# RWKV layer: r read from PSUM by its users, and the first half's preparation issued per head pair beside the r projection

## The chip, the cores and the metric

The kernel runs on one core of a Trainium2 chip. The metric is the device time of one execution in microseconds (us). A core has five engines that run their own queues in order and wait for each other by semaphores: TensorE (PE, with its weight loads PEld), VectorE (DVE), ScalarE (ACT), GpSimd (POOL) and SyncE (SP), which issues the loads.

## The reference, cut to what matters

The program is a chain of two blocks on 512 tokens of width 1024: an RWKV-7 time mix, an MLP, an attention layer, a second MLP, and then a block with a gated delta rule, latent attention and experts. Only the RWKV time mix is touched by the change. It has 16 heads of 64.

```
r, k, v = xr @ wr, xk @ wk, xv @ wv
decay = exp(-exp(w_log));  a = sigmoid(...)
kk = k * k_k, normalised per head
k  = k * (1 + (a - 1) * k_a)
for t:  S = S diag(decay_t) + (S (-kk_t)) (kk_t a_t)^T + v_t k_t^T;   y_t = S r_t
bonus = sum over a head of (r * k * r_k)
```

The recurrence is computed in eight chunks of 64 tokens. Within a chunk a triangular matrix of key products per head is inverted, so that the chunk's steps become matrix products.

## The kernel before, in words

Everything is feature-major: a tile of 128 partitions by 512 tokens holds two heads, a head pair p of 0 to 7. A projection goes through `dense_fm`, which for each p loads 128 columns of the weight, splits them into a high part on ScalarE (L181) and a low part on VectorE (L183), and issues 24 matmuls (L244 to L246) into one PSUM bank. The bank is handed to a function `use`.

For the r projection `use_r` keeps one pair back and calls `make_r` (L656 and on) on the pair before. `make_r` copies r from PSUM to SBUF on ScalarE (L659), makes the decay factors W and 1/W with two exponentials (L664, L666), and then the operands of the pair. On VectorE: kkn (L671, which reads the spread norm from PSUM), kp (L677), the bonus product of r (L679), and for each half of the sequence (four chunks) the two parts of `ar` (L689 from kkn, L690 from r). On GpSimd: kka (L673) and the two parts of `bk` (L691, L692). `sum_bonus` (L652) multiplies the bonus product on TensorE.

After the projection the weights' pool is closed, a pool `rwb` opens in its room, and `prepare(0)` runs over the eight pairs of the first half (chunks 0 to 3). For each pair: two modulation steps (`self.spare(2)`, a load of 512 KB from SP and matmuls L342, transposes L345 on VectorE); eight score matmuls (L729) into two PSUM banks; masks that write the scores into the matrix tile `GB` (L738, VectorE) and into the operands (L749 on VectorE, or L751 on ScalarE and L752 on GpSimd); a scaled copy of `bk` (L761 on ScalarE or L756 on GpSimd), its transposes (L765) and a copy out of PSUM (L767). Then the matrices are transposed in 32x32 blocks (L777), and the diagonal blocks of all 16 heads are inverted in 62 small steps (L783, L785), on VectorE in the first half and on GpSimd in the second. After that come transposes back (L793, L796) and block products on TensorE (L801, L808). `prepare(1)` does the same for chunks 4 to 7. Its pairs and inverse are traced behind everything else (`self.behind(100000)`) and write their matrix with L741 on ScalarE and L742 and L743 on GpSimd. The chunk loop (L902 to L939) follows; chunk 4 needs the second half's blocks.

PSUM has eight banks: five of tag "b", two of tag "f", one of tag "m" (modulation). In this layer `self.ps()` gives a "b" bank; under `behind` it gives an "f" bank. SBUF tiles of 128x512 come from one pool of 59 slots. A scheduler fixes each engine's order when the program is built: it issues what is ready by its own estimate of time, the earlier traced first.

Of the kernel before, what the change touches and what calls it, by code (L numbers as in the profile page):

```python
# [122 lines left out]
class K:  # L123
# [392 lines left out]
    def rwkv(self, x_dram, G, sh, gt, xT):  # L516
        nc, tc, A = self.nc, self.tc, self.A
        C0 = float(_np.exp(-0.5))
        self.open_weights(1024)
        rstd = self.rstd_fm(xT)  # L520
        hT, xx = [], []
        for k in range(KT):
            t = self.s()
# [113 lines left out]
        AR = [[None, None] for _ in range(8)]  # L637
# [17 lines left out]

        def make_r(p, pt):  # L656
            rB = spr(p)
            r = self.s()
            nc.scalar.activation(r, pt, AF.Copy)  # L659
            cum, aa = CA[p]  # L660
            CA[p] = None
            W = self.wp.tile([128, 8, 65], F32, name=self.nm("W"), tag="w65")
            nc.gpsimd.memset(W[:, :, 0:1], 1.0)
            nc.scalar.activation(W[:, :, 1:65], cum.rearrange("p (c t) -> p c t", t=64), AF.Exp, scale=-C0)  # L664
            Wi = self.s()
            nc.scalar.activation(Wi, cum, AF.Exp, scale=C0)  # L666
# [12 lines left out]
            nc.vector.scalar_tensor_tensor(prod, r, self.col("rw_rk", p), kp, op0=OP.mult, op1=OP.mult)  # L679
            prods.append((p, prod))  # L680
            if p:
                sum_bonus(*prods.pop(0))
            v3 = lambda x, hf: x[:, hf * 256:hf * 256 + 256].rearrange("p (c t) -> p c t", t=64)
            for hf in range(2):
                ar, bk = self.s(), self.s()
                AR[p][hf], BK[p][hf] = ar, bk
                a4, b4 = (z.rearrange("p (c t) -> p c t", t=128) for z in (ar, bk))
                cs = slice(hf * 4, hf * 4 + 4)
                nc.vector.scalar_tensor_tensor(a4[:, :, 0:64], v3(kkn, hf), -1.0, W[:, cs, 0:64], op0=OP.mult, op1=OP.mult)  # L689
                nc.vector.tensor_tensor(a4[:, :, 64:128], v3(r, hf), W[:, cs, 1:65], op=OP.mult)  # L690
                nc.gpsimd.tensor_tensor(b4[:, :, 0:64], v3(kka, hf), v3(Wi, hf), op=OP.mult)  # L691
                nc.gpsimd.tensor_tensor(b4[:, :, 64:128], v3(kp, hf), v3(Wi, hf), op=OP.mult)  # L692

        self.dense_fm(A["rw_wr"], xr, 0, D, use_r)
# [6 lines left out]
        gm = self.cst("gmask")  # L701
        idn = self.cst("ident")
        Y = [[None, None] for tt in range(4)]
        with tc.tile_pool(name="rwb", bufs=2, side="right", reuse_waits="tile") as bp:
            def new_sv(c):
# [4 lines left out]
                    out.append(t)  # L710
                return out

            X, BKt, GB = [None, None], [None, None], [None, None]

            def prepare(hf):
                eng = nc.gpsimd if hf else nc.vector
                GBh = bp.tile([128, 32, 128], F32, name=self.nm("GB"), tag="gb")
                Xh = [None] * 16
                Bh = [None] * 8
                for p in range(8):  # L720
                    g = p // 4
                    ar, bk = AR[p][hf], BK[p][hf]
                    self.spare(0 if hf else 2)
                    pts = [self.ps(), self.ps()]
                    for ci in range(4):
                        cs = slice(ci * 128, ci * 128 + 128)
                        for hd in range(2):
                            q = slice(hd * 64, hd * 64 + 64)
                            nc.tensor.matmul(pts[hd][:, cs], bk[q, cs], ar[q, cs], start=(ci == 0), stop=(ci == 3),  # L729
                                             skip_group_check=True)  # L730
                    xo = self.s()
                    nc.scalar.activation(xo[0:64], ar[64:128], AF.Copy)
                    for hd in range(2):
                        u0 = ((2 * p + hd) % 8) * 4
                        v = pts[hd].rearrange("p (c t) -> p c t", t=128)
                        o = GBh[g * 64:g * 64 + 64, u0:u0 + 4, :]
                        if hf == 0:
                            nc.vector.tensor_tensor(o, v[0:64], gm[0:64].unsqueeze(1).to_broadcast([64, 4, 128]), op=OP.mult)  # L738
                        else:

                            nc.scalar.activation(o, v[0:64], AF.Copy)  # L741
                            nc.gpsimd.memset(o[32:64, :, 0:32], 0.0)  # L742
                            nc.gpsimd.tensor_tensor(o[:, :, 64:128], o[:, :, 64:128],  # L743
                                                    gm[g * 64:g * 64 + 64, 64:128].unsqueeze(1).to_broadcast([64, 4, 64]), op=OP.mult)
                        dst = ar if hd == 0 else xo
                        d3 = dst[64:128].rearrange("p (c t) -> p c t", t=128)
                        mk = gm[64:128].unsqueeze(1).to_broadcast([64, 4, 128])
                        if hf == 0 and hd == 0:
                            nc.vector.tensor_tensor(d3, v[64:128], mk, op=OP.mult)  # L749
                        else:  # L750
                            nc.scalar.activation(d3, v[64:128], AF.Copy)  # L751
                            nc.gpsimd.tensor_tensor(d3, d3, mk, op=OP.mult)  # L752
                    Xh[2 * p], Xh[2 * p + 1] = ar, xo
                    dg = self.s()
                    if hf == 0 and p % 2:
                        nc.gpsimd.tensor_tensor(dg.rearrange("p (c t) -> p c t", t=128), bk.rearrange("p (c t) -> p c t", t=128),  # L756
                                                WCp[:, p, hf * 4:hf * 4 + 4].unsqueeze(2).to_broadcast([128, 4, 128]), op=OP.mult)
                    else:
                        for ci in range(4):
                            cs = slice(ci * 128, ci * 128 + 128)  # L760
                            nc.scalar.activation(dg[:, cs], bk[:, cs], AF.Copy, scale=WCp[:, p, hf * 4 + ci:hf * 4 + ci + 1])  # L761
                    pt = self.ps()
                    for ci in range(4):
                        cs = slice(ci * 128, ci * 128 + 128)
                        nc.tensor.transpose(pt[:, cs], dg[:, cs], idn)  # L765
                    Bh[p] = self.s()
                    nc.scalar.activation(Bh[p], pt, AF.Copy)  # L767

                P = bp.tile([128, 32, 32], F32, name=self.nm("P"), tag="p4", bufs=2)
# [25 lines left out]
                for ub in range(0, 32, 16):  # L797
# [15 lines left out]
                X[hf], BKt[hf], GB[hf] = Xh, Bh, GBh  # L813

            def finish(tt, g):

# [57 lines left out]
            step = lambda n, m: [next(z, None) for z in [gt8] * n + [bn8] * m]  # L874
            pr1 = prepare(1)
            with self.behind(100000, slots=False):
                next(pr1)
            SV = [new_sv(0), new_sv(1)]
            for g in range(2):
# [65 lines left out]
                        step(GA_[c], GB_[c])  # L945
            step(8, 8)
            del sv, us, z, zy


        self.need(1)  # L950
# [1463 lines left out]
```

## Time and profile before

| | |
|---|---|
| median of 3 runs | 3014.67 us (3011.07 to 3020.56) |
| the profiled execution's own time | 3021.37 us |
| its span in the profile | 3019.6 us |
| TensorE busy | 2778.8 us, 92% |
| VectorE / ScalarE / GpSimd busy | 1627.1 / 1051.5 / 732.4 us |
| mean granted TensorE clock | 0.952 |

Times in the rows are microseconds from the start of the span; the mean of one instruction in a group is in nanoseconds. "Idle before" is the time in which an engine had nothing running just ahead of the instructions of a group, with what ended it. PEclk is the granted clock of TensorE as a share of full speed. Matmuls are pipelined, so their busy times overlap.

### The profile page before, as it was taken

How to read it: one execution, taken by the hardware profiler on the slowest of the kernel's cores; microseconds unless marked ns; L12 is line 12 of the kernel's file. 1: busy time of each engine (PE TensorE's matmuls, PEld its weight loads, DVE VectorE, ACT ScalarE, POOL GpSimd, SP SyncE). 2: the span in 40 equal slices, each digit the busy share in tenths (PEclk: the TensorE clock that was granted, in tenths of full speed). 3: DMA queues.
4: the chain of work that ended last, by engine and by line, in shares of the span. 5: the costliest groups of instructions: out<-in, count | busy, mean ns of one | idle time of the engine just before them, and what ended most of it. 6: DMA issues, size and time to landing. Idle time of an engine off the chain costs nothing.

```text
span 3019.6 us, 38042 instructions
## 1 busy us (share of the span) xinstructions
PE 2778.8 (92%) x15046; PEld 1975.0 (65%) x15046; DVE 1627.1 (54%) x2449; ACT 1051.5 (35%) x1711; POOL 732.4 (24%) x563
## 2 busy tenths in 40 slices
PE   5998888999999999999999998898799997999997
PEld 1665466788877777788886776666677884444433
DVE  4568855456673447566536779638765542112112
ACT  2454533422234457432223452253335322110001
POOL 2446453211111034121113453134242121000000
PEclk8997777999999999999999999999999998999999
DMA  6322514256573321455532324142253359899998
GB/s 206 118 70 83 159 56 163 89 167 189 185 240 98 96 70 45 136 176 179 176 98 65 105 70 119 54 133 66 64 178 92 101 189 356 340 386 409 409 409 307
DMA packets 361011, 502.05 MB, mean 166 GB/s; under 512 B 24769, under 2 KB 236993, under 8 KB 360833
## 3 DMA queue, kind: packets, MB, share of 16 engines
q1 hardware_dynamic: 349600, 479.01, 46.9%
q10 hardware_dynamic: 11232, 20.62, 1.9%
q8 instruction: 118, 1.93, 0.3%
q14 instruction: 61, 0.49, 0.1%
HBM read 471.26 MB, written 26.21 MB: 165 GB/s over the span
## 4 chain that ended last, share of the span: by engine, by line
PE 68%; DVE 19%; DMA 5%; ACT 3%; issue 3%; POOL 2%; SPq 0%; ACTq 0%; DVEq 0%; POOLq 0%
PE psb L244 10%; PE psb L246 10%; PE psb L245 10%; PE psb L2114 5%; PE psb L1303 4%; PE psb L2142 4%; PE psf L1303 2%; DMA rg<-in_w_up_dram 2%; DMA rg<-in_w_gate_dram 1%; PE psb L1204 1%; PE psm L342 1%; DVE s L1465 1%; DVE tm L1380 1%; DVE R L1389 1%; DVE tm L1387 1%
## 5 line engine op out<-in xcount | busy, mean ns | idle before, releaser
L244 PE MATMUL psb<-s,wh 128*128 128x512 f32 x1384 | 543.6, 393 | 2.7 <-DVE s L968 1.9
L245 PE MATMUL psb<-s,wl 128*128 128x512 f32 x1384 | 541.6, 391 | 2.4 <-DVE wl L183 2.3
L246 PE MATMUL psb<-s,wh 128*128 128x512 f32 (+1 forms) x1320 | 514.8, 390 | 1.3 <-POOL s L481 0.6
L181 ACT ACTIVATE wh<-wr 128x1024 fp32r<-128x1024 f32 (+1 forms) x221 | 288.1, 1305 | 397.7 <-PE psb L246 263.9
L183 DVE TENSOR_TENSOR wl<-wr,wh 128x1024 fp32r<-128x1024 f32 (+1 forms) x145 | 257.2, 1775 | 262.9 <-ACT wh L181 259.5
L244 PEld LDWEIGHTS psb<-s,wh 128*128 128x128 f32 x1384 | 260.0, 188 | 70.9 <-issue 9.8
L245 PEld LDWEIGHTS psb<-s,wl 128*128 128x128 f32 x1384 | 259.9, 188 | 59.6 <-DVE wl L183 3.1
L246 PEld LDWEIGHTS psb<-s,wh 128*128 128x128 f32 (+1 forms) x1320 | 247.4, 188 | 58.0 <-issue 2.9
L183 POOL TENSOR_TENSOR wl<-wr,wh 128x1024 fp32r<-128x1024 f32 (+1 forms) x76 | 186.7, 2460 | 395.7 <-ACT wh L181 376.2
L2114 PE MATMUL psb<-rg,s 128*64 128x512 f32 x1024 | 242.9, 597 | 5.1 <-DMA rg<-in_w_up_dram 3.8
L1303 PE MATMUL psf<-f,wh 128*128 128x512 f32 (+1 forms) x688 | 232.0, 411 | 10.7 <-ACT wh L181 10.7
L999 POOL TENSOR_TENSOR s<-s 128x512 f32<-128x512 f32 x64 | 101.1, 1580 | 515.9 <-ACT s L997 436.6
L2114 PEld LDWEIGHTS psb<-rg,s 128*64 128x64 f32 x1024 | 83.0, 136 | 142.2 <-issue 120.7
L1303 PEld LDWEIGHTS psf<-f,wh 128*128 128x128 f32 (+1 forms) x688 | 133.2, 195 | 42.7 <-ACT wh L181 11.5
L1303 PE MATMUL psf<-f,wl 128*128 128x512 f32 (+1 forms) x344 | 143.1, 416 | 16.5 <-POOL wl L183 16.4
L2142 PE MATMUL psb<-rg,s 128*64 128x512 f32 (+1 forms) x544 | 129.6, 620 | 0.1
L378 DVE SCALAR_TENSOR_TENSOR mt<-mr,crep,mt 128x512 f32<-128x512 f32 x168 | 126.5, 753 | 3.6
L201 ACT ACTIVATE s<-s 128x512 fp32r<-128x512 f32 x112 | 69.7, 625 | 138.0 <-POOL s L999 73.2
L1006 DVE SCALAR_TENSOR_TENSOR s<-psb,aff,s 128x512 f32<-128x512 f32 x64 | 45.9, 751 | 129.7 <-PE psb L246 129.7
L1303 PE MATMUL psb<-f,wh 128*128 128x512 f32 (+1 forms) x336 | 106.4, 396 | 7.8 <-DVE f L479 5.9
L997 ACT ACTIVATE s<-psb 128x512 f32<-128x512 f32 x64 | 37.6, 588 | 164.0 <-PE psb L246 164.0
L2142 PEld LDWEIGHTS psb<-rg,s 128*64 128x64 f32 x544 | 46.1, 147 | 74.2 <-issue 68.8
(569 smaller groups left out, 4968.4 us busy)
## 6 DMA issues: line engine op xcount, KB each, us to landing
rg<-in_w_gate_dram SPq DMA_DIRECT2D x64, 1024.0 KB
rg<-in_w_up_dram SPq DMA_DIRECT2D x64, 1024.0 KB
rg<-in_w_down_dram SPq DMA_DIRECT2D x64, 1024.0 KB
mr<-in_mod_w_dram SPq DMA_DIRECT2D x96, 512.0 KB
wr<-in_mlp_down_dram SPq DMA_DIRECT2D x32, 1024.0 KB
wr<-in_mlp_up_dram SPq DMA_DIRECT2D x31, 1024.0 KB
wr<-in_w_in_dram SPq DMA_DIRECT2D x54, 512.0 KB
mr<-in_w_mod_dram SPq DMA_DIRECT2D x40, 512.0 KB
```

The costliest lines, as they stand in the source:

```text
L181: nc.scalar.activation(hi, raw, AF.Copy)
L183: (lo_eng or self.lo_eng or nc.vector).tensor_tensor(lo, raw, hi.bitcast(F32), op=OP.subtract)
L201: nc.scalar.activation(hi, src, AF.Copy)
L244: nc.tensor.matmul(pt[:mw], hi[k][:, j:j + mw], a, start=(k == 0), stop=False)
L245: nc.tensor.matmul(pt[:mw], lo[k][:, j:j + mw], a, start=False, stop=False)
L246: nc.tensor.matmul(pt[:mw], hi[k][:, j:j + mw], b, start=False, stop=(k == nk - 1))
L378: nc.vector.scalar_tensor_tensor(acc[:, hb], raw[:, d], c, acc[:, hb], op0=OP.mult, op1=OP.add)
L999: nc.gpsimd.tensor_tensor(sq, r, r, op=OP.mult)
L1006: nc.vector.scalar_tensor_tensor(xT[m], pt, gt[:, m:m + 1], xT[m], op0=OP.mult, op1=OP.add)
L1303: nc.tensor.matmul(pt[:rows, :cols], x, y, start=(k == 0 and q == 0), stop=(k == nk - 1 and q == 2))
L2114: nc.tensor.matmul(B[n][q], XE[hp][k0 // 2][:, o:o + 64], w[e][:, k, n * 512:n * 512 + 512], start=(k0 + k == 0), stop=(k0 + k == 7), skip ...
L2142: last = nc.tensor.matmul(pt[q, :n], HT[(k + i) // 4][:, o:o + 64], w[e][i], start=(k + i == 0), stop=(k + i == 7), skip_group_check=True)
```

## The change

Three things change in the RWKV layer, and two numbers elsewhere. `make_r` no longer copies r; L679 and the two L690 read the PSUM bank. The loop over pairs in `prepare` becomes a generator `pairs(hf, pool)`; the first half's generator is advanced by one pair after each `make_r` from the second on, so that six of its eight pairs are traced inside the r projection, and the last two behind it. Its score matmuls take "f" banks. The first half's matrix `GB` lies in a pool of its own, opened ahead of the weights' pool; `rwb` keeps one such buffer instead of two. The copy of the bonus comes after the eighth pair. The number of slots goes from 59 to 58, and the scratch for DMA descriptors from its default to 1 KB per partition.

```diff
     def rwkv(self, x_dram, G, sh, gt, xT):
+        gbm = tc.tile_pool(name="gb0", bufs=1, side="right", reuse_waits="tile")
+        gb0 = gbm.__enter__()
         self.open_weights(1024)
...
             if p:
                 make_r(*held.pop(0))
+            if p > 1:
+                prep[0].send(None)
...
             rB = spr(p)
-            r = self.s()
-            nc.scalar.activation(r, pt, AF.Copy)
...
-            nc.vector.scalar_tensor_tensor(prod, r, self.col("rw_rk", p), kp, op0=OP.mult, op1=OP.mult)
+            nc.vector.scalar_tensor_tensor(prod, pt, self.col("rw_rk", p), kp, op0=OP.mult, op1=OP.mult)
...
-                nc.vector.tensor_tensor(a4[:, :, 64:128], v3(r, hf), W[:, cs, 1:65], op=OP.mult)
+                nc.vector.tensor_tensor(a4[:, :, 64:128], v3(pt, hf), W[:, cs, 1:65], op=OP.mult)
...
+        def pairs(hf, pool):
+            GBh = GB[hf] = pool.tile([128, 32, 128], F32, name=self.nm("GB"), tag="gb", bufs=1)
...
+                self.spare(0 if hf else 2)
+                pts = [self.bank("f"), self.bank("f")]
...
+                Bh[p] = self.s()
+                nc.scalar.activation(Bh[p], pt, AF.Copy)
+                yield
+
+        prep = [pairs(0, gb0)]
         self.dense_fm(A["rw_wr"], xr, 0, D, use_r)
         make_r(*held.pop(0))
+        prep[0].send(None)
         sum_bonus(*prods.pop(0))
+        self.run(prep[0])
         nc.scalar.activation(bonus, pbon[:, 0:64].rearrange("p (c h) -> p c h", h=16), AF.Copy)
         self.close_weights()
...
             with self.behind(100000, slots=False):
+                self.run(pairs(1, bp))
                 next(pr1)
...
-            self.begin(st, 59)
+            self.begin(st, 58)
...
-    nc = _bacc.Bacc("TRN2", target_bir_lowering=False, num_devices=1)
+    nc = _bacc.Bacc("TRN2", target_bir_lowering=False, num_devices=1, dynamic_dma_scratch_size=1024)
```

What stands between these lines in `pairs` is the loop body of `prepare`, moved word for word.

## Rows read from the trace of the kernel before

**Rows 1.** The page: busy time of the engines, share of the span and instructions (first line), and the DMA queues that carry data with packets, megabytes and share of 16 engines.

```profile
PE 2778.8 (92%) x15046; PEld 1975.0 (65%) x15046; DVE 1627.1 (54%) x2449; ACT 1051.5 (35%) x1711; POOL 732.4 (24%) x563
...
q1 hardware_dynamic: 349600, 479.01, 46.9%
q10 hardware_dynamic: 11232, 20.62, 1.9%
```

**Rows 2.** Busy time by stretch: from to, length, busy us and instructions of PE, PEld, DVE, ACT, POOL, granted clock, DMA share, GB/s. The first stretch is the r projection's, the second the first half's preparation up to its inverse.

```profile
203.40:265.80 62.40, 53.05 (x249) 42.38 (x247) 59.37 (x73) 22.57 (x37) 47.18 (x52) 0.87 0.11 32
265.80:304.75 38.95, 32.78 (x211) 18.13 (x210) 27.09 (x38) 22.19 (x47) 19.77 (x20) 0.77 0.50 174
```

**Rows 3.** VectorE's groups by form from 203.4 to 304.75 us: line, operation, output and inputs, shapes, count, busy us, mean ns of one, idle before.

```profile
L690 DVE TENSOR_TENSOR s<-s,W 128x256 f32<-128x256 f32 x16 | 13.0, 813 | 0.0
L679 DVE SCALAR_TENSOR_TENSOR s<-s,P,s 128x512 f32<-128x512 f32 x8 | 11.1, 1388 | 0.4
L738 DVE TENSOR_TENSOR GB<-psb,C 64x512 f32<-64x512 f32 x16 | 10.8, 682 | 11.3 <-PE psb L729 11.1
...
L671 DVE SCALAR_TENSOR_TENSOR s<-s,P,psb 128x512 f32<-128x512 f32 x8 | 5.9, 743 | 0.4 <-PE psb L303 0.3
L749 DVE TENSOR_TENSOR s<-psb,C 64x512 f32<-64x512 f32 x8 | 5.6, 695 | 0.2
```

**Rows 4.** VectorE in order of time from the matrix transposes on: start, duration, instruction, count.

```profile
300.68 3.96 DVE L777 STREAM_TRANSPOSE P<-GB 32x1024 f32<-32x1024 f32 x2
304.75 0.20 DVE L783 TENSOR_TENSOR tm<-P,R 128x31 f32<-128x31 f32 x1
...
347.96 4.05 DVE L793 STREAM_TRANSPOSE TT<-R 32x1024 f32<-32x1024 f32 x2
...
368.26 3.86 DVE L777 STREAM_TRANSPOSE P<-GB 32x1024 f32<-32x1024 f32 x2 [3.02 <-PE psb L801]
```

**Rows 5.** GpSimd in order of time: the first and the last mask of the second half's pairs, and the first and the last step of the second half's inverse.

```profile
306.69 0.20 POOL L742 MEMSET GB<- 32x128 f32 x1 [2.56 <-ACT GB L741]
...
366.05 1.26 POOL L752 TENSOR_TENSOR s<-s,C 64x512 f32<-64x512 f32 x1
...
378.07 0.68 POOL L783 TENSOR_TENSOR tm<-P,R 128x31 f32<-128x31 f32 x1 [4.58 <-DVE P L777]
...
419.48 0.25 POOL L785 TENSOR_TENSOR R<-R,tm 128x31 f32<-128x31 f32 x1
```

**Rows 6.** The chain of work that ended last, in order of time: the last products of chunk 3 and the first of chunk 4.

```profile
415.18 1.09 PE psb L934 x16
...
437.54 0.84 PE psb L902 x12
```

**Rows 7.** Busy time by stretch, columns as in rows 2: dense stages behind the RWKV layer, and the end with the experts.

```profile
500.00:1000.00 500.00, 485.43 (x2160) 380.90 (x2161) 291.53 (x327) 168.57 (x195) 83.99 (x53) 0.99 0.52 166
...
2400.00:3019.00 619.00, 566.08 (x2597) 287.20 (x2595) 141.37 (x222) 98.53 (x153) 33.25 (x27) 0.96 0.89 345
```

**Rows 8.** VectorE in order of time in the r stage: two instructions of the same form.

```profile
219.00 0.41 DVE L690 TENSOR_TENSOR s<-s,W 128x256 f32<-128x256 f32 x1
...
224.16 0.94 DVE L690 TENSOR_TENSOR s<-s,W 128x256 f32<-128x256 f32 x1
```

**Rows 9.** GpSimd in order of time around these two.

```profile
217.56 0.91 POOL L692 TENSOR_TENSOR s<-s,s 128x256 f32<-128x256 f32 x1
219.48 0.12 POOL L663 MEMSET W<- 128x8 f32 x1 [1.01 <-DVE s L690]
...
223.92 0.91 POOL L691 TENSOR_TENSOR s<-s,s 128x256 f32<-128x256 f32 x1
```

**Rows 10.** VectorE's groups by form over the whole span: an instruction of another layer with a 128x256 input in PSUM.

```profile
L1180 DVE CUSTOM_DVE_ANT_0 s<-psb,mask 128x256 f32<-128x256 f32 x16 | 6.7, 417 | 10.5 <-PE psb L1175 10.5
```

**Rows 11.** TensorE in order of time: the first and the last matmul of one tile of a projection (of k; r's have the same form), the last of the third r tile, the first scores of the second half, a pair's bonus sums, and a modulation group, transposes and scores of one pair of the first half.

```profile
138.39 0.50 PE L244 MATMUL psb<-s,wh 128*128 128x512 f32 x1
...
143.78 0.40 PE L246 MATMUL psb<-s,wh 128*128 128x512 f32 x1
...
206.44 0.40 PE L246 MATMUL psb<-xl,wh 128*128 128x512 f32 x1
...
210.42 0.71 PE L729 MATMUL psf<-s,s 64*128 64x128 f32 x6
...
223.89 0.95 PE L652 MATMUL psb<-C,s 128*128 128x2 f32 x8
...
279.10 1.06 PE L342 MATMUL psm<-mr,crep 128*32 128x512 f32 x8
280.10 0.66 PE L765 MATMUL psb<-C,s 128*128 128x128 f32 x4
280.68 1.16 PE L729 MATMUL psb<-s,s 64*128 64x128 f32 x16
```

**Rows 12.** Waits of SyncE's queue from 150 to 440 us: line, what it waited for, total us, times, longest. L328 loads the modulation weights, L179 the projection weights.

```profile
SPq L328 <- PE psm L342: 101.1, 19, 48.9
SPq L179 <- DVE wl L183: 56.9, 9, 11.8
```

**Rows 13.** Waits from 203 to 270 us: ScalarE.

```profile
ACT W L664 <- DVE s L690: 30.4, 6, 6.1
```

**Rows 14.** ScalarE in order of time: the first copies of the second half's scores into its matrix.

```profile
266.45 1.05 ACT L741 ACTIVATE GB<-psf 64x512 f32<-64x512 f32 x2
```

More of the change, by code (lines that the diff above doesn't have):

```diff
@@ L689, in make_r @@
                 nc.vector.scalar_tensor_tensor(a4[:, :, 0:64], v3(kkn, hf), -1.0, W[:, cs, 0:64], op0=OP.mult, op1=OP.mult)
-                nc.vector.tensor_tensor(a4[:, :, 64:128], v3(r, hf), W[:, cs, 1:65], op=OP.mult)
+                nc.vector.tensor_tensor(a4[:, :, 64:128], v3(pt, hf), W[:, cs, 1:65], op=OP.mult)
                 nc.gpsimd.tensor_tensor(b4[:, :, 0:64], v3(kka, hf), v3(Wi, hf), op=OP.mult)
                 nc.gpsimd.tensor_tensor(b4[:, :, 64:128], v3(kp, hf), v3(Wi, hf), op=OP.mult)
+        gm = self.cst("gmask")
@@ new lines, in rwkv @@
+        idn = self.cst("ident")
+        X, BKt, GB = [None, None], [None, None], [None, None]
+        def pairs(hf, pool):
+            GBh = GB[hf] = pool.tile([128, 32, 128], F32, name=self.nm("GB"), tag="gb", bufs=1)
+            Xh = X[hf] = [None] * 16
+            Bh = BKt[hf] = [None] * 8
+            for p in range(8):
+                g = p // 4
+                ar, bk = AR[p][hf], BK[p][hf]
+                self.spare(0 if hf else 2)
+                pts = [self.bank("f"), self.bank("f")]
+                for ci in range(4):
+                    cs = slice(ci * 128, ci * 128 + 128)
+                    for hd in range(2):
+                        q = slice(hd * 64, hd * 64 + 64)
+                        nc.tensor.matmul(pts[hd][:, cs], bk[q, cs], ar[q, cs], start=(ci == 0), stop=(ci == 3),
+                                         skip_group_check=True)
+                xo = self.s()
+                nc.scalar.activation(xo[0:64], ar[64:128], AF.Copy)
+                for hd in range(2):
+                    u0 = ((2 * p + hd) % 8) * 4
+                    v = pts[hd].rearrange("p (c t) -> p c t", t=128)
+                    o = GBh[g * 64:g * 64 + 64, u0:u0 + 4, :]
+                    if hf == 0:
+                        nc.vector.tensor_tensor(o, v[0:64], gm[0:64].unsqueeze(1).to_broadcast([64, 4, 128]), op=OP.mult)
+                    else:
+                        nc.scalar.activation(o, v[0:64], AF.Copy)
+                        nc.gpsimd.memset(o[32:64, :, 0:32], 0.0)
+                        nc.gpsimd.tensor_tensor(o[:, :, 64:128], o[:, :, 64:128],
+                                                gm[g * 64:g * 64 + 64, 64:128].unsqueeze(1).to_broadcast([64, 4, 64]), op=OP.mult)
+                    dst = ar if hd == 0 else xo
+                    d3 = dst[64:128].rearrange("p (c t) -> p c t", t=128)
+                    mk = gm[64:128].unsqueeze(1).to_broadcast([64, 4, 128])
+                    if hf == 0 and hd == 0:
+                        nc.vector.tensor_tensor(d3, v[64:128], mk, op=OP.mult)
+                    else:
+                        nc.scalar.activation(d3, v[64:128], AF.Copy)
+                        nc.gpsimd.tensor_tensor(d3, d3, mk, op=OP.mult)
+                Xh[2 * p], Xh[2 * p + 1] = ar, xo
+                dg = self.s()
+                if hf == 0 and p % 2:
+                    nc.gpsimd.tensor_tensor(dg.rearrange("p (c t) -> p c t", t=128), bk.rearrange("p (c t) -> p c t", t=128),
+                                            WCp[:, p, hf * 4:hf * 4 + 4].unsqueeze(2).to_broadcast([128, 4, 128]), op=OP.mult)
+                else:
+                    for ci in range(4):
+                        cs = slice(ci * 128, ci * 128 + 128)
+                        nc.scalar.activation(dg[:, cs], bk[:, cs], AF.Copy, scale=WCp[:, p, hf * 4 + ci:hf * 4 + ci + 1])
+                pt = self.ps()
+                for ci in range(4):
+                    cs = slice(ci * 128, ci * 128 + 128)
+                    nc.tensor.transpose(pt[:, cs], dg[:, cs], idn)
+                Bh[p] = self.s()
+                nc.scalar.activation(Bh[p], pt, AF.Copy)
+                yield
@@ L694, in rwkv @@
+        prep = [pairs(0, gb0)]
         self.dense_fm(A["rw_wr"], xr, 0, D, use_r)
         make_r(*held.pop(0))
+        prep[0].send(None)
         sum_bonus(*prods.pop(0))
+        self.run(prep[0])
         nc.scalar.activation(bonus, pbon[:, 0:64].rearrange("p (c h) -> p c h", h=16), AF.Copy)
         self.close_weights()
-        gm = self.cst("gmask")
-        idn = self.cst("ident")
         Y = [[None, None] for tt in range(4)]
@@ L711, in new_sv @@
                 return out
-            X, BKt, GB = [None, None], [None, None], [None, None]
             def prepare(hf):
                 eng = nc.gpsimd if hf else nc.vector
[L717 to L767, printed above, removed]
@@ L771, in prepare @@
+                GBh = GB[hf]
                 P = bp.tile([128, 32, 32], F32, name=self.nm("P"), tag="p4", bufs=2)
@@ L811, in prepare @@
                         nc.scalar.activation(GBh[q0, ub:ub + 16, 32:64], pt[q0].rearrange("p (u j) -> p u j", j=32), AF.Copy)
-                X[hf], BKt[hf], GB[hf] = Xh, Bh, GBh
             def finish(tt, g):
@@ L947, in rwkv @@
             del sv, us, z, zy
+        gbm.__exit__(None, None, None)
         self.need(1)
```

## The prediction

> **What bounds the kernel now.** I read the page first: TensorE is busy 92% of the span [rows 1], so a change in VectorE or ScalarE work matters only where TensorE waits for them. The change lies in the RWKV layer, so I cut that layer into stretches [rows 2]. From 203.4 us, where the first head pair's vectors are made, to 304.75, where the first half's triangular inverse starts, VectorE is busy 59.4 + 27.1 = 86.5 of 101.4 us, while TensorE is granted 0.87 and 0.77 of its full clock: it is the waiting engine here.
>
> Then I took VectorE's groups by form in these 101 us [rows 3]. In the r stage (to 265.8) it has no idle time worth a name. In the preparation (265.8 to 304.75) it loses 11.3 us ahead of L738, for score matmuls that come late. So the time from the r projection to the inverse is VectorE's work, 86.5 us, plus 14.9 us of waiting.
>
> What follows the inverse start is a chain: inverse of half one (to 348), block products, transposes of half two's matrices at 368.3 [rows 4], half two's inverse on GpSimd from 378.1 to 419.7 [rows 5], and chunk 4 at 437.5, although chunk 3 had finished at 416.3 [rows 6]. Half two's inverse, not the chunks 0 to 3, sets when chunk 4 starts; it waits for half one's block products (its transposes go into buffers that these free) and for half two's own pairs, whose masks lie from 306.7 to 367.3 [rows 5], behind the transposes of half one at 300.7. So an inverse that starts earlier by G moves both, and the rest of the program behind them: the dense stages after it have TensorE busy 485 of 500 us, and the experts' stage at the end, with DMA at 0.89 [rows 7], begins behind them and not at a fixed time. I therefore take G as the gain of the whole.
>
> **r read from PSUM.** It removes eight ScalarE copies. ScalarE is not a bound, so I give nothing for them. It changes the source of one L679 and two L690 per head pair. L690 takes 0.41 us in one place and 0.94 in another, same form and shape [rows 8]; the mean is 0.813, that of L679 1.388 [rows 3]. The short one falls between two instructions of GpSimd, the long one beside its L691 [rows 9]. L671, which has one PSUM input and the same 128x512 shape as L679, has 0.743 as its mean in the same stretch, beside the same GpSimd work [rows 3]. A VectorE instruction with a 128x256 PSUM input takes 0.417 elsewhere [rows 10]. So I price L679 at 0.743 and L690 at 0.417: 8 x (1.388 - 0.743) + 16 x (0.813 - 0.417) = 5.2 + 6.3 = 11.5 us. The bounds: nothing gained if PSUM reads suffer like SBUF reads; 11.5 is the upper end, because 0.41 is also the shortest L690 seen. I take the upper end, since the eight L671 average 0.743 beside the same neighbour; with nothing gained here the sum below would give 3008.8.
>
> A rule speaks against this. The Trainium skill (Perfetto Trace Analysis, Optimizing Scalar/DVE Operations) gives VectorE about 60 ns of access overhead per instruction on SBUF and about 125 ns on PSUM; by that rule alone 24 instructions would lose 24 x 65 ns, an estimate of 1.6 us from that page, and the gain would be a loss. The trace does not bear it out here (0.417 against the undisturbed 0.41), so its part in rival 5 is small.
>
> The price of the edit is a PSUM bank: r's bank was freed by the copy at the start of a pair's vectors and is now held to their end, some 6 us more, out of five "b" banks (the bonus sum, r of this pair, r of the next, the spread norm, and now a preparation transpose). TensorE can run one head pair ahead instead of two.
>
> **Preparation beside the r projection.** Nothing is removed; it moves. Per pair VectorE gets 2 x 0.682 + 0.695 = 2.06 us [rows 3]. The score and transpose matmuls, ScalarE copies and GpSimd masks move along, and so do the modulation steps that each pair calls: two steps per pair, their matmuls 1.06 us at full clock [rows 11], and their 16 weight loads of 512 KB on SP's queue, past the r weights. That queue waits 56.9 us for L183 and 101.1 us for L342 in 150 to 440 us [rows 12], so a modulation load can sit behind a weight load; three steps are loaded ahead, and the r weights one tile ahead, so I cost it at nothing; it would cost one pair's period, about 9 us, if a load were needed at once.
>
> Does the r stage have room? VectorE: after the saving, 75.0 us of work remain from 203.4 to the inverse. TensorE: three r tiles are done at 206.4; five remain at 5.6 us (24 matmuls of the same form, the first and the last of a tile in the rows), 28 us; and eight times bonus 0.95, scores 1.16, transposes 0.66 and modulation 1.06, together 31 us [rows 11]. So 59 us at full clock, to 265; at the granted 0.87, 68 us, to 274. VectorE without idle would be through the last pair at 203.4 + 75.0 - 3.96 = 274.4. The two are equal at that clock, so they will wait for each other.
>
> Idle left on VectorE: the r stage's own 3.0 us stay; the two pairs that are left behind the projection keep 11.9 / 8 x 2 = 3.0 us; for TensorE being late in the six others I take 3 us (between 0 and the 9 that the old rate for six pairs gives). Sum 9.
>
> **Smaller edits.** The descriptor scratch: the page's data moves on two hardware queues [rows 1], none that GpSimd fills, so nothing. The matrix of half one in a pool of its own lets the pairs write while the r weights are still held; that is what allows the move. 58 slots for 59: a slot is missing, if at all, in chunks 0 to 3, which hold most; those have 437.5 - 416.3 = 21 us before chunk 4 [rows 6], so nothing.
>
> **Sum.** 203.4 + 75.0 + 9 = 287.4 instead of 304.75: G = 17.4 us. Against its own time, 3021.4, that is 3004.0; this execution lies above the median, 3014.7, and from the median it is 2997.3, which I forecast.
>
> **Rivals.**
> 1. All waits hidden but the r stage's 3.0 and 1 us at the end: 203.4 + 79 = 282.4, G = 22.4, 2992.3. For it: ScalarE and GpSimd have room. Against: TensorE's 274 us at 0.87, with nothing to spare.
> 2. The pairs lag. Two "f" banks serve them instead of five "b". Half two's pairs, on these two banks, took (367.3 - 306.7) / 8 = 7.6 us each [rows 5], half one's (300.7 - 265.8) / 8 = 4.4 [rows 4]. ScalarE, in order, waits at L664 for the last L690 of a pair two back, up to 6.1 us at a time [rows 13], with the copies that free an "f" bank behind it. If five pairs are left behind the r projection, VectorE's end of r is 265.8 - 11.5 + 3 x 2.06 = 260.5, and 5 x 7.6 + 3.96 follow: 302.4, G = 2.3, 3012.4; four left give 296.9, G = 7.9, 3006.8. The Trainium skill (Perfetto Trace Analysis, Matmuls) asks that independent groups rotate through different banks, so that one is emptied while the next is filled; by that rule this would be the case to expect. The rows bear it out for half two's pairs only, where two more ScalarE copies per pair empty the banks.
> 3. Slower. Half two's first pair put its scores into both "f" banks at 210.4 [rows 11], and its copy to the matrix, which needs room that the weights pool gives up, came at 266.5 [rows 14]. Before, nobody else wanted "f". If the new order does this again ahead of half one's second pair, all eight pairs wait for the end of r: 265.8 - 11.5 + 8 x 7.6 + 3.96 = 319.1, 14.3 us later, 3029. It decides if a score of half two is issued before half one's last. Against it: half one's scores come first in the program's order and are ready first.
> 4. No passage: G is reached at the inverse but lost before chunk 4, because half two's pairs, with 7.6 us each and the modulation, still end near 367. Then 3014.7. Against: in the trace they begin right behind half one's.
> 5. PSUM reads are no shorter beside GpSimd: the first term is nothing, G = 5.9, 3008.8. Against: L671.
>
> **Chances and numbers.** Forecast 0.52 (idle of 6 to 14.9 us: G from 20.4 down to 11.5, 2994 to 3003); rival 1 0.14; rival 2 0.13; rival 3 0.10; rival 4 0.07; rival 5 0.04. The runs shown spread over 9.5 us, so about 0.3%, 9 us, is what a measurement tells from no change. Faster: 0.52 + 0.14 + 0.04 of rival 2, 0.70. Slower: rival 3, 0.10. Same: the rest, 0.20. The range goes from 2990 (rival 1, less 2 us for the spread) to 3015 (rivals 2, 4 and 5) and leaves out rival 3 and the tails.
>
> **What would show it.** L679 near 0.74 and L690 near 0.42 in the profile after; L738 between the L690 of the r stage; six of eight pairs' L738 before the last L690; the first inverse step 17 us earlier on VectorE, GpSimd's first step and chunk 4 by the same. L690 at 0.8 would break the first term; a long wait ahead of L738, or TensorE's clock at 0.7 in the r stage, the third; "f" scores of half two ahead of half one's last would show rival 3.

## The result: slower, by 0.4 to 0.7 per cent

The changed kernel took 3037.02 us (median of four runs, 3032.97 to 3038.30), the kernel before 3017.61 us on the same chip. The ratio is 1.0057, with a 95% interval of 1.0041 to 1.0074: 12 to 22 us slower. The forecast was 2997.3 us, faster.

The page's first line, as in [rows 1], and then the busy times and the clock by stretch, columns as in [rows 2]: the first stretch of [rows 2], and the one with the last matrix transposes ahead of the inverse.

```profile
PE 2777.4 (92%) x15046; PEld 1980.8 (65%) x15046; DVE 1619.0 (53%) x2449; ACT 1049.7 (35%) x1703; POOL 727.1 (24%) x563
```
```profile
203.40:265.80 62.40, 45.54 (x243) 33.29 (x242) 39.27 (x64) 21.30 (x36) 32.76 (x39) 0.83 0.28 93
...
303.00:316.15 13.15, 12.27 (x50) 8.36 (x42) 11.28 (x10) 7.01 (x17) 5.58 (x7) 0.50 0.25 80
```

Against [rows 1] no engine has more to do; VectorE has 8 us less. Yet in the 62.4 us of the first stretch VectorE is busy for 39.3 us where it was 59.4 [rows 2], and TensorE for 45.5 instead of 53.1. Both do less per time: they wait for each other. In the second stretch, where before the inverse was under way from 304.75 on, TensorE is granted 0.50.

VectorE's groups by form from 200 to 316 us, as in [rows 3], and then the waits from 200 to 305 us.

```profile
L723 DVE TENSOR_TENSOR GB<-psf,C 64x512 f32<-64x512 f32 x16 | 10.9, 682 | 2.5 <-PE psf L714 2.2
L691 DVE SCALAR_TENSOR_TENSOR s<-s,W 128x256 f32<-128x256 f32 x16 | 10.5, 655 | 0.0
...
L692 DVE TENSOR_TENSOR s<-psb,W 128x256 f32<-128x256 f32 x16 | 6.5, 409 | 0.0
L673 DVE SCALAR_TENSOR_TENSOR s<-s,P,psb 128x512 f32<-128x512 f32 x8 | 6.0, 748 | 37.5 <-PE psb L303 37.5
L681 DVE SCALAR_TENSOR_TENSOR s<-psb,P,s 128x512 f32<-128x512 f32 x8 | 5.9, 742 | 0.1
```
```profile
DVE s L673 <- PE psb L303: 37.5, 8, 8.1
...
PE psb L656 <- DVE s L681: 24.0, 7, 4.6
```

The lines have moved: kkn is L673 (was L671), the bonus product L681 (L679), the r part of `ar` L692 (L690), the kkn part L691 (L689), the masks L723 (L738), the scores L714 (L729), the bonus sum L656 (L652), the pairs' transposes L750 (L765). The two reads of r are as short as forecast. What is new is the idle time ahead of kkn: 0.4 us in [rows 3], 37.5 us now, all of it for L303, the matmul that spreads a pair's norm over its partitions. The kkn part of the kernel before, from the view of [rows 3], stands here for comparison:

```profile
L689 DVE SCALAR_TENSOR_TENSOR s<-s,W 128x256 f32<-128x256 f32 x16 | 14.6, 915 | 0.0
```

One pair's period in TensorE's order of time shows why. Of the r tile's 24 matmuls only the first and the last stand here. Below it, VectorE's rows of the same period.

```profile
221.32 0.39 PE L303 MATMUL psb<-s,s 128*128 128x512 f32 x1
221.64 1.16 PE L714 MATMUL psf<-s,s 64*128 64x128 f32 x16
227.43 1.81 PE L656 MATMUL psb<-C,s 128*128 128x2 f32 x8 [4.62 <-DVE s L681]
229.17 1.93 PE L342 MATMUL psm<-mr,crep 128*32 128x512 f32 x8
231.03 1.11 PE L750 MATMUL psb<-C,s 128*128 128x128 f32 x4
231.80 0.78 PE L244 MATMUL psb<-s,wh 128*128 128x512 f32 x1
...
238.39 0.40 PE L246 MATMUL psb<-xl,wh 128*128 128x512 f32 x1
238.63 0.39 PE L303 MATMUL psb<-s,s 128*128 128x512 f32 x1
```
```profile
221.75 0.75 DVE L673 SCALAR_TENSOR_TENSOR s<-s,P,psb 128x512 f32<-128x512 f32 x1 [5.91 <-PE psb L303]
...
226.64 0.73 DVE L681 SCALAR_TENSOR_TENSOR s<-psb,P,s 128x512 f32<-128x512 f32 x1
...
239.13 0.75 DVE L673 SCALAR_TENSOR_TENSOR s<-s,P,psb 128x512 f32<-128x512 f32 x1 [8.14 <-PE psb L303]
```

Follow the chain: the spread norm at 221.3 releases VectorE's kkn; 4.9 us later VectorE comes to the bonus product L681 (ahead of it stand, among others, the low part of a weight tile, L183 with 2.33 us, and a mask of the moved preparation); TensorE has stood for 4.62 us with the bonus sum L656 at the head of its queue, waiting for that product; behind the bonus sum stand modulation, transposes, 7.0 us of an r tile, and only then the next pair's spread norm, for which VectorE has by now waited 8.14 us. Each engine runs while the other stands, and a pair takes 17.4 us (221.75 to 239.13); before, the first two pairs lay 7.7 us apart (kkn at 203.40 and 211.10), without the preparation, and with it the two stages took 101.4 / 8 = 12.7 us per pair. The kernel before issued its r tile and spread norm ahead of the bonus sum, so that its bonus sums waited 5.0 us in all, from 200 to 305 us:

```profile
PE psb L652 <- DVE s L679: 5.0, 3, 3.5
```

The standing costs twice, as the granted clock shows: TensorE's wait, what follows it, and the later part of the r tile.

```profile
222.80:227.43 4.63, 0.01 (x2) 0.01 (x1) 4.63 (x5) 1.16 (x2) 3.92 (x4) 1.00 0.26 73
227.43:233.40 5.97, 5.97 (x24) 4.00 (x25) 3.49 (x8) 1.76 (x4) 2.68 (x5) 0.51 0.27 75
234.44:238.63 4.19, 4.19 (x20) 3.39 (x18) 0.00 (x0) 0.00 (x0) 0.97 (x1) 1.00 0.25 98
```

After 4.6 us without work the clock is at 0.51, the lower level of 1.2 GHz, for about 6 us, in which the work takes twice as long (L656 1.81 us instead of 0.95, L342 1.93 instead of 1.06 [rows 11]): some 3 us in this pair.

From the stretch to the end the delay passes as the prediction said a gain would. VectorE's inverse of half one, GpSimd's of half two, and chunk 4 on TensorE:

```profile
316.15 0.20 DVE L792 TENSOR_TENSOR tm<-P,R 128x31 f32<-128x31 f32 x1
```
```profile
388.00 0.68 POOL L792 TENSOR_TENSOR tm<-P,R 128x31 f32<-128x31 f32 x1 [4.57 <-DVE P L786]
```
```profile
449.34 0.91 PE L910 MATMUL psb<-s,s 128*64 128x64 f32 x12
```

They are 11.4, 9.9 and 11.8 us later than in [rows 4], [rows 5] and [rows 6], and the span is 11.6 us longer (3031.2 for 3019.6). The stretch itself has grown by more, since this execution began it 3.3 us earlier (first kkn at 200.11 instead of 203.40): 116.0 us from the first kkn to the inverse, where it was 101.4, so 14.7 us. That is inside the 12 to 22 us of the medians. This length is used below, because it is free of when an execution reaches the stretch.

### The profile page after: what moved, and what is told of

It is laid out like the page before. It is cut to its first block, busy times and chain, and to the rows that moved or that the text cites. A ratio compares the mean times of both kernels' runs of the same rounds, so it can differ in the third digit from the quotient of the medians.

```text
span 3031.2 us, 38070 instructions
## 1 busy us (share of the span) xinstructions
PE 2777.4 (92%) x15046; PEld 1980.8 (65%) x15046; DVE 1619.0 (53%) x2449; ACT 1049.7 (35%) x1703; POOL 727.1 (24%) x563
## 3 DMA queue, kind: packets, MB, share of 16 engines
q8 instruction: 118, 1.93, 0.3%
## 5 line engine op out<-in xcount | busy, mean ns | idle before, releaser
L181 ACT ACTIVATE wh<-wr 128x1024 fp32r<-128x1024 f32 (+1 forms) x221 | 288.2, 1305 | 415.3 <-PE psb L246 266.1
L183 DVE TENSOR_TENSOR wl<-wr,wh 128x1024 fp32r<-128x1024 f32 (+1 forms) x145 | 260.1, 1795 | 261.3 <-ACT wh L181 261.0
L183 POOL TENSOR_TENSOR wl<-wr,wh 128x1024 fp32r<-128x1024 f32 (+1 forms) x76 | 185.8, 2447 | 397.6 <-ACT wh L181 378.8
```

Of the source, the lines that this page charges most:

```text
L181: nc.scalar.activation(hi, raw, AF.Copy)
L183: (lo_eng or self.lo_eng or nc.vector).tensor_tensor(lo, raw, hi.bitcast(F32), op=OP.subtract)
```

## The experiments

The theory grew in the runs. At first it was the PSUM banks: in the built program the pairs' transposes keep one "b" bank for themselves and the bonus sum another, so that the r tile of pair p+2 gets the bank that the spread norm of p had, and the spread norm of p+1 the bank of r of p. This is read from the programs; the traces do not tell one bank from another. Rivals: r's bank is held too long; the move of the pairs itself is dear; the slots. All runs in one table, ratio to the kernel before on the same chip:

| kernel | r | pairs' transposes | wait of kkn for L303, us | first kkn to inverse, us | chunk 4 starts, us | ratio (95% interval) |
|---|---|---|---|---|---|---|
| before | copied | after the r stage | 0.3 | 101.4 | 437.5 | 1 |
| changed | PSUM | beside, "b" | 37.5 | 116.0 | 449.3 | 1.0057 (1.0041 to 1.0074) |
| e1 | PSUM | after | 0.8 | 86.1 | 422.0 | 0.9936 (0.9920 to 0.9953) |
| e2 | copied | beside, "b" | 37.7 | 126.9 | 462.2 | 1.0075 (1.0063 to 1.0086) |
| e3 | copied | after; 58 slots, 1 KB | none listed | 101.2 | 436.8 | 0.9998 (0.9990 to 1.0006) |
| e4 | PSUM | beside, "f" | 6.1 | 89.6 | 415.3 | 0.9925 (0.9913 to 0.9937) |
| e5 | copied | beside, "f" | 1.4 | 93.9 | 419.4 | 0.9945 (0.9931 to 0.9958) |
| e8 | PSUM | beside, "b"; bonus sum behind | 18.8 | 99.4 | 429.2 | 0.9981 (0.9970 to 0.9992) |
| e9 | PSUM | as e4, four masks moved | 1.3 | 88.0 | 419.4 | 0.9962 (0.9949 to 0.9975) |
| e10 | PSUM | after; bonus in two banks | 2.2 | 88.3 | 421.5 | 0.9949 (0.9932 to 0.9965) |
| e11 | copied | after; bonus in two banks | 0.3 | 98.0 | 430.6 | 0.9979 (0.9967 to 0.9990) |
| e12 | PSUM | beside, "b"; both behind | 3.9 | 78.2 | 412.0 | 0.9910 (0.9893 to 0.9926) |

Waits are those between 200 and 305 us.

**e1: r from PSUM alone.** The three edits of `make_r`, in the kernel before.

```diff
-            r = self.s()
-            nc.scalar.activation(r, pt, AF.Copy)
...
-            ... scalar_tensor_tensor(prod, r, ...)
+            ... scalar_tensor_tensor(prod, pt, ...)
...
-            ... v3(r, hf) ...
+            ... v3(pt, hf) ...
```

> The kernel before, with r read from PSUM by its users and nothing else of the change. Theory (the pairs' transposes take the fifth "b" bank, so that an r tile waits for the end of an earlier pair's vectors): without pairs in the r stage four banks do, TensorE still runs a tile ahead, the wait of VectorE for the spread norm stays below 3 us, the r stage ends about 11.5 us earlier and the time falls by 8 to 12 us (ratio 0.996 to 0.997). Rival (holding r's bank longer is enough by itself): the wait for the spread norm rises to 10 us and more here too, and the time is the same or up to 10 us longer.

Measured: 3001.52 us, 0.9936, and a wait of 0.8 us. Holding r's bank longer is harmless by itself. The gain, 19 us by the ratio and 15.3 us in the stretch, is larger than either theory had it. VectorE's groups from 203 to 305 us (L687 is the kkn part, L688 the r part, L736 the mask, L677 the bonus product):

```profile
L687 DVE SCALAR_TENSOR_TENSOR s<-s,W 128x256 f32<-128x256 f32 x16 | 11.4, 710 | 0.0
L736 DVE TENSOR_TENSOR GB<-psb,C 64x512 f32<-64x512 f32 x16 | 10.9, 682 | 7.3 <-PE psb L727 7.0
...
L688 DVE TENSOR_TENSOR s<-psb,W 128x256 f32<-128x256 f32 x16 | 6.6, 412 | 0.0
L677 DVE SCALAR_TENSOR_TENSOR s<-psb,P,s 128x512 f32<-128x512 f32 x8 | 6.0, 751 | 0.5
```

Beside the 11.5 us of the two r reads (412 and 751 ns against 813 and 1388 [rows 3]) the kkn part fell from 915 to 710 ns, 3.3 us, though its own operands did not change, and the idle time ahead of the masks from 11.3 to 7.3 us. Against that, kp (L675 here) rose from 1028 to 1191 ns.

**e2: the pairs beside the projection, r copied again** (the changed kernel with the copy put back).

> The changed kernel with the copy of r to SBUF put back, so that r's bank is free early and the pairs still run beside the projection. Rival (r's bank held to the end of the pair's vectors is what delays the next r tile): the wait of VectorE for the spread norm falls from 37.5 to below 10 us, and the time comes to 3000 to 3015. Theory (the pairs' transposes and the order of TensorE's queue that goes with them: bonus sum, modulation, transposes, then the r tile and the spread norm): the wait stays at 20 us or more, VectorE's own work is 11.5 us longer, and the time is 3025 to 3045.

Measured: 3042.22 us, 1.0075. The wait stays, in the same two lines:

```profile
DVE s L675 <- PE psb L303: 37.7, 6, 8.9
...
PE psb L656 <- DVE s L683: 24.5, 6, 5.3
```

So it is not r's bank: freeing it early changes nothing in the wait, and VectorE's work grows again. The loss belongs to the move of the pairs, as it stands in the queue.

**e3: 58 slots and the small scratch alone.**

```diff
-            self.begin(st, 59)
+            self.begin(st, 58)
...
+    nc = _bacc.Bacc(..., dynamic_dma_scratch_size=1024)
```

> The kernel before, with 58 slots instead of 59 and the scratch of 1 KB alone. Theory: no difference (ratio 0.999 to 1.001). Rival (a missing slot delays a chunk or a later layer): 3 to 17 us longer.

Measured: 0.9998. Nothing, as forecast.

**e4: the pairs' transposes in an "f" bank**, so that a "b" bank is free.

```diff
-                pt = self.ps()
+                pt = self.bank("f")
                 for ci in range(4):
...
                     nc.tensor.transpose(pt[:, cs], dg[:, cs], idn)
```

> The changed kernel, with the pairs' transposes in an "f" bank instead of a "b" bank; r is still read from PSUM. Theory (the transposes take the fifth "b" bank): the r tile and the spread norm go ahead of the bonus sum in TensorE's queue, the wait for the spread norm falls from 37.5 to below 10 us, the inverse of half one starts at 285 to 300 us instead of 316, and the time is 2998 to 3012, unless three uses of two "f" banks per pair hold the pairs back. Rival (the move of the pairs itself, with scores and modulation in TensorE's queue, costs the time): the wait stays above 20 us and the time at 3025 to 3045.

Measured: 2998.66 us, 0.9925; one word turns the change from a loss of 17 us into a gain of 23. The wait for the spread norm is 6.1 us, and TensorE's granted clock from 203.4 to 265.8 us is 1.00. In the built program the r tile and the spread norm now stand ahead of the bonus sum. That left two explanations entangled: a bank more, and another order in TensorE's queue.

```profile
DVE s L673 <- PE psb L303: 6.1, 6, 1.7
```

**e8: the order alone.** The changed kernel, transposes in "b", r tiles in the same banks; only the bonus sum is tied behind the next pair's spread norm.

```diff
             rB = spr(p)
+            mark = self.last_pe()
...
             if p:
-                sum_bonus(*prods.pop(0))
+                with self.tc.issue_after(mark):
+                    sum_bonus(*prods.pop(0))
```

> The changed kernel, its transposes still in a "b" bank, with each pair's bonus sum tied to a place in TensorE's queue behind the spread norm of the next pair; nothing else is changed, and the r tiles take the same banks as in the changed kernel. Theory (the place in the queue costs most: the bonus sum waits for a product late in VectorE's pair, and the r tile and the next spread norm stand behind it): no wait of TensorE for L681 is left, VectorE's wait for the spread norm falls from 37.5 to 10 to 22 us, the inverse of half one starts at 293 to 306 us, and the time is 3002 to 3018. Rival (the bank alone: the r tile comes late wherever the bonus sum stands): the wait stays above 28 us and the time at 3025 to 3040.

Measured: 3013.64 us, 0.9981. TensorE no longer waits for the product, and the wait for the spread norm is halved. What is left of it has a new head of the queue, seen in the waits from 200 to 305 us and in TensorE's order of time:

```profile
DVE s L674 <- PE psb L303: 18.8, 7, 7.3
...
PE psb L752 <- POOL W L666: 11.4, 2, 6.2
```
```profile
222.80 1.11 PE L752 MATMUL psb<-C,s 128*128 128x128 f32 x4 [6.19 <-POOL W L666]
```

L752 are a pair's transposes. The profile puts the release down to L666, a short instruction of GpSimd at 222.69, but the data comes from the one before it: in the odd pairs the scaled copy (L743 here) is GpSimd's, and it stands there behind the next pair's products. GpSimd in order of time:

```profile
220.66 0.90 POOL L696 TENSOR_TENSOR s<-s,s 128x256 f32<-128x256 f32 x1
221.53 1.22 POOL L743 TENSOR_TENSOR s<-s,WCp 128x512 f32<-128x512 f32 x1
222.69 0.11 POOL L666 MEMSET W<- 128x8 f32 x1
```

Behind the transposes stand the r tile and the spread norm.

**e10 and e11: the bank alone.** The bonus sums in two "b" banks instead of one, in e1 and in the kernel before. No pair is moved.

```diff
-        pbon = self.ps()
+        pbon = [self.ps(), self.ps()]
...
-                nc.tensor.matmul(pbon[:, tt * 16 + 2 * p:tt * 16 + 2 * p + 2], prod...
+                nc.tensor.matmul(pbon[tt // 2][:, tt % 2 * 16 + 2 * p:tt % 2 * 16 + 2 * p + 2], prod...
```

> The kernel before with r read from PSUM (no pairs moved), and with the bonus sums in two "b" banks instead of one, half the columns in each. That takes a fifth "b" bank as the pairs' transposes do, with no other work: the r tiles and the spread norms take the same banks in turn as in the changed kernel, and the bonus sums stand behind the spread norm. Theory (the shortage by itself only makes the spread norm wait for the end of the pair before; what makes it dear is what TensorE's queue has between the two): VectorE's wait for the spread norm is 0.4 to 1 us per pair, 3 to 8 us in all, and the time is 2 to 7 us above that of r from PSUM alone (ratio 0.994 to 0.996). Rival (the missing bank alone accounts for most): the wait is 15 us or more and the time 10 to 20 us above it (0.997 to 1.001).

> The kernel before, unchanged but for the bonus sums in two "b" banks. r is still copied to SBUF, which frees its bank at the start of the pair. Theory: the copy gives the bank back in time, the wait for the spread norm stays below 5 us and the time within 5 us of before (ratio 0.998 to 1.002). Rival (a fifth bank in use is dear with or without the copy): 10 us and more above before.

Measured: e10 0.9949, with a wait of 2.2 us, against e1's 0.8 and below the theory's 3 to 8; the intervals of the two ratios overlap. e11 0.9979, no loss with the copy either (why it is 6 us below the kernel before was not followed up).

```profile
DVE s L669 <- PE psb L303: 2.2, 4, 1.2
```

By the order in which the program asks for banks, those of e10 rotate as in the changed kernel, and it costs next to nothing. The first theory falls in its plain form: without the pairs beside the projection the missing bank does not take the time. With them, it is e12 that decides.

**e12: the order, all of it.** e8, and each pair's transposes traced one pair later, behind the next spread norm and bonus sum, when their copies have long been made. All five "b" banks stay in use.

```diff
+        def turn(Bh, p, dg, mark):
+            pt = self.ps()
+            with (self.tc.issue_after(mark) if mark is not None else contextlib.nullcontext()):
+                for ci in range(4):
...
+                    nc.tensor.transpose(pt[:, cs], dg[:, cs], idn)
+            Bh[p] = self.s()
+            nc.scalar.activation(Bh[p], pt, AF.Copy)
...
+                if hf == 0 and late:
+                    turn(Bh, *late.pop(0), self.last_pe())
+                if hf == 0 and p < 7:
+                    late.append((p, dg))
+                else:
+                    turn(Bh, p, dg, None)
                 yield
```

> The changed kernel with the bonus sum tied behind the next pair's spread norm, and with a pair's transposes traced one pair later, when their scaled copies have long been made; they stay in a "b" bank, and all five are in use. Theory (what waits in TensorE's queue in front of the r tile is the cost, first the bonus sum, then the transposes that wait for copies; the shortage of banks costs little by itself): the wait for the spread norm falls from 18.8 to below 8 us, the inverse of half one starts at 287 to 293 us, and the time is 2996 to 3006 (ratio 0.992 to 0.996). Rival (the rest of the wait is the missing bank): the wait stays at 12 us or more, the inverse starts at 296 or later, and the time is above 3008.

Measured: 2996.41 us, 0.9910, the lowest ratio of all, though its interval touches e4's. Its wait from 200 to 305 us, one period on TensorE (L709 are the transposes, L727 the scores), the stretch of [rows 2], and the first step of the inverse:

```profile
DVE s L674 <- PE psb L303: 3.9, 5, 1.4
```
```profile
225.19 0.40 PE L303 MATMUL psb<-s,s 128*128 128x512 f32 x1
225.52 1.07 PE L342 MATMUL psm<-mr,crep 128*32 128x512 f32 x8
226.51 1.05 PE L656 MATMUL psb<-C,s 128*128 128x2 f32 x8
227.50 1.16 PE L727 MATMUL psf<-s,s 64*128 64x128 f32 x16
228.59 0.66 PE L709 MATMUL psb<-C,s 128*128 128x128 f32 x4
229.00 0.48 PE L244 MATMUL psb<-s,wh 128*128 128x512 f32 x1
...
234.62 0.40 PE L303 MATMUL psb<-s,s 128*128 128x512 f32 x1
```
```profile
203.40:265.80 62.40, 61.34 (x395) 44.82 (x394) 55.86 (x95) 30.69 (x52) 50.55 (x58) 1.00 0.41 129
```
```profile
278.56 1.28 DVE L805 TENSOR_TENSOR tm<-P,R 128x31 f32<-128x31 f32 x1
```

The same instructions as in the changed kernel, the same number of banks, no wait at the head of the queue: 9.4 us per pair instead of 17.4, TensorE busy for 61.3 of 62.4 us at the full clock, the stretch 38 us shorter. Not all of this arrives: against e4 the stretch is 11.4 us shorter, but from the first kkn to chunk 4 only 4.7 us are left (211.7 and 216.4), because the way from the inverse to chunk 4 takes 133.4 us here and 126.8 in e4.

**e5: the move alone, with the transposes in "f" and r copied** (e2 and e4's edit together).

> The changed kernel with the copy of r to SBUF put back and the pairs' transposes in an "f" bank: the move of the pairs alone, without the shortage of "b" banks. Theory (VectorE's work bounds the stretch, so that moving the pairs gives only the idle time that it takes away, and the PSUM reads give the rest): the inverse of half one starts at 296 to 304 us, and the time is 0 to 9 us below that of the kernel before (ratio 0.997 to 1.000). Rival (the move of the pairs is what gains, the PSUM reads give little): the inverse starts near 289 and the time is 2996 to 3004.

Measured: 3002.38 us, 0.9945: between the two theories in the stretch (7.4 us shorter), and as fast as the rival in time. Each edit alone gains 17 to 19 us, and both together in e4 only 23. A further 5.9 us of e5's gain, and of e4's, lie between the start of the inverse and chunk 4: 126.8 us in both (292.59 to 419.40, 288.49 to 415.29), 132.7 before (304.75 to 437.47). In e4's trace 3.7 of them lie between half one's transposes back (L793 before) and half two's matrix transposes (L777), 16.6 us where it was 20.3, and 2.0 between these and GpSimd's first step, 7.8 where it was 9.8. Why these two steps are shorter was not traced.

**e9: is e4 bound by VectorE?** Four of its masks moved to ScalarE and GpSimd.

```diff
-                    if hf == 0 and hd == 0:
+                    if hf == 0 and hd == 0 and p % 2:
                         nc.vector.tensor_tensor(d3, v[64:128], mk, op=OP.mult)
```

> The changed kernel with the transposes in an "f" bank, and for the even pairs the mask of L734 moved from VectorE to ScalarE and GpSimd (the way the second head of a pair goes already). Theory (VectorE bounds the stretch with 69.8 of 85.5 us): four masks of 0.695 us less, and the time 2 to 4 us below that with the transposes in "f" alone (2995 to 2997). Rival (the two "f" banks and GpSimd's masks are as close a bound): no gain or up to 8 us longer.

Measured: 3008.38 us, 0.9962, 10 us slower than e4 and beyond both expectations. The stretch is 1.6 us shorter, of the 2.8 us taken from VectorE; VectorE is not e4's only bound. From the first kkn to chunk 4 it is 1.9 us longer (218.3 against 216.4). The rest of the 10 us lies outside: this execution reaches the first kkn 2.2 us later and needs 5.8 us more behind the start of chunk 4. Where that arises stays open.

## Why the prediction was wrong, point by point

**What bounds the kernel.** Right in the main: the stretch sets the end. In the changed kernel its 14.7 us are passed on, and in e12 its gain of 23.1 us comes out as 27 us by the ratio. It is no rule of one for one: e4 has 11.8 us from the stretch and 23 by the ratio, and e9 loses against e4 with a shorter stretch.

**r from PSUM, 11.5 us.** Right, within 8 ns: 409 for the forecast 417, 742 for 743. It was too small in what it left out, the kkn part L691, which fell from 915 to 655 ns (4.2 us) with both its operands still in SBUF. Rival 5 is out. The rule weighed in the prediction, on a longer access to PSUM (the Trainium skill, Perfetto Trace Analysis, Optimizing Scalar/DVE Operations), does not show here: 409 ns from PSUM against 0.41 us for the undisturbed read from SBUF [rows 8]. The r part averages 409 to 412 ns wherever it reads PSUM, and 711 in e2, 752 in e5, 813 before, where it reads two SBUF tiles. One by one, four of the sixteen before have no GpSimd tensor instruction beside them and take 0.41 us, the other twelve take 0.94 to 0.96; in the changed kernel thirteen of the sixteen have one beside them, and all take 0.41. That agrees with the Trainium skill (SBUF — State Buffer, Who interferes with whom), which says that a VectorE instruction with two SBUF inputs contends with a GpSimd instruction that reads SBUF and one with at most one does not; that the kkn part profits too is not in it. All sixteen kkn parts of the changed kernel run beside GpSimd and take 0.41 to 0.81 us, where fifteen of sixteen took 0.94 to 0.96 before; why was not isolated here.

**The bank, priced at nothing.** As a price of the bank alone this was nearly right: 2.2 us in e10. As an argument it stopped too early. "TensorE can run one head pair ahead instead of two" should have led to the next question: what then stands in front of the r tile and the spread norm in TensorE's queue, and for whom does that wait? The prediction did not ask it of its own move.

**"For TensorE being late in the six others I take 3 us (between 0 and the 9 that the old rate for six pairs gives)."** This is the step that failed: for the 3 us the trace has 37.5. From the first kkn to the inverse VectorE worked 73.6 us, where 75.0 were forecast, and stood 42.4, where 9 were forecast; in e12 it works 71.3 and stands 6.9. The term's upper end was no bound. The old 11.3 us were measured in the preparation stage, where TensorE waited for no product of the pair's vectors; beside the projection a pair's bonus sum hangs on VectorE, VectorE's next pair on the spread norm, and the spread norm on the queue. The capacity estimate (TensorE to 274 us at the granted 0.87, VectorE to 274.4) concluded that they would "wait for each other" and then priced that at 3 us. Capacity was not the trouble: in e12 the same work runs at a clock of 1.00 in the first 62 us. It also took the clock as given, though it depends on the waits (0.83 in the changed kernel, 1.00 in e4 and e12, over the same 62.4 us).

**Loads.** Right: no wait of the modulation matmuls for a load is among the waits of this stretch. ScalarE stands 14.0 us ahead of the r weights' high parts (L181), of which VectorE's L183 sees 0.2.

**Slots and scratch, nothing.** Right (e3).

**Sum.** 84.0 us from the first kkn to the inverse were forecast. With the order mended it is 78.2 (e12), a little less than rival 1's 79.0; with the bank freed 89.6 (e4); as the change stands 116.0.

**Rivals.** Rival 3 (3029) has the right sign and size by luck, with the wrong mechanism: its mark, a score of half two ahead of half one's last, is absent, and the first mask of half two on GpSimd (L727) comes at 314.27, behind the last of half one (in the kernel before it came at 306.69 [rows 5]). Rival 2, two "f" banks too few for the pairs, is absent as well: the masks wait 2.5 us for their scores. The rule it named (the Trainium skill, Perfetto Trace Analysis, Matmuls: let independent groups rotate through different banks) was near the matter, but e10 and e12, with all five "b" banks in use and waits of 2.2 and 3.9 us, show that here the order of what waits decides. Rival 4 is out: half two and chunk 4 followed the inverse by nearly the same amount (9.9 and 11.8 us for 11.4). The true case, a lock step through TensorE's queue, was not among the rivals.

## What to carry to other kernels

When work is moved beside another stage, write down the order of the in-order engine there, and ask of each moved instruction whom it waits for and what stands behind it; a short matmul that waits for a late product can hold a whole projection. A sum of busy times is reached only if that order lets the engines overlap, and an idle time measured in one stage is no upper end for the same work in another. And separate a shortage from its consequence: the missing bank by itself, with no pairs moved, came with 2 us of waiting, the queue order that followed from it with 37.5, and moving two small groups back in the queue took nearly all of that away.

## What the runs showed of the hardware that was not expected

An SBUF-only VectorE instruction became shorter when its neighbours read PSUM: the kkn part, with both operands in SBUF, went from 915 ns to 710 (e1) and 655 (changed kernel). With r copied again it is 785 (e2) and 806 (e5), and there most of those beside a GpSimd instruction take 0.94 us or more, as before.

Waiting costs clock: after one wait of 4.6 us TensorE's granted clock was 0.51 for the next 6 us, and 1.00 again in the later part of the same r tile. Removing the waits raised the clock of the stretch from 0.83 to 1.00, above the 0.87 of the kernel before.
